# The in-place sums of weights of a decoder layer move from VectorE to GpSimd

## The chip, the cores and the metric

The kernel runs on one core of one Trainium2 chip. The metric is the device time of one execution in microseconds. The core's engines have their own instruction queues: TensorE (PE, its weight loads PEld), VectorE (DVE), ScalarE (ACT), GpSimd (POOL) and SyncE (SP). They wait for each other by semaphores. DMAs are issued from the queues of SP, ACT and POOL.

## The reference

One layer of a decoder for 512 tokens of width 1024, in float32:

```
h   = rmsnorm(x, ln1) @ w_in       # columns: GLA q,k,v,r, forget gate; 3 groups of attention q,k,v; 2 gates
A   = gated linear attention (4 heads, chunks of 64)  -> norm, silu gate, @ w_o_gla
B   = causal dilated windowed attention (3 groups of 4 heads), combined by softmax weights, @ w_o_attn
x  += (sigmoid(gA) * A + sigmoid(gB) * B) @ w_out
x  += relu(rmsnorm(x, ln2) @ w_mlp1)^2 @ w_mlp2      # 1024 -> 4096 -> 1024
x  += sigmoid(rmsnorm(x, ln3) @ w_pg) * (p @ w_pp)
out = rmsnorm(x, ln_f)
```

Nearly all of the work is products of 512 x 1024 activations with weights of 1024 rows or more.

## The kernel before, in words

**Products in three parts.** Each float32 operand is split into a rounded high part `hi` and a rest `lo`, and TensorE forms hi*hi + hi*lo + lo*hi. A weight operand is a tile of 128x1024. ScalarE makes its `hi` (L280), VectorE its `lo` = w - `hi` (L275, both operands in SBUF).

**Seven products in place of eight.** Most weights are taken in groups in the manner of Strassen: four blocks A11, A21, A12, A22 give the seven weight operands A11, S1 = A21 + A22, A22, S2 = S1 + A11, A12, S4 = S2 + A12 and S3 = A11 + A21. `strassen` runs the seven stages in the order of STAGES, one operand a stage, 24 products of 256 columns each; `wide` does the same with two tiles per operand (S2.0, S2.1 and so on) and products of 512 columns. There are 22 groups of the first kind (k1, q2, k2, v0, gq, gk, gb0, gb1, ga0, ga1, m1q0 to m1q7 for w_mlp1, and m2s0c1, m2s1c1, m2s0c3, m2s1c3 for w_mlp2) and 3 of the second (v12, gv, r).

**How the sums are made.** S1 is one DMA from SP and a second from POOL that adds onto it (L242). S2 and S4 are made in place in S1's buffer by VectorE: in `sums`, L254 and L260 for the first kind, L251 for `wide`. S3 is made in A11's buffer by an adding DMA from POOL (L257), after S2 has read A11. There are 22 + 22 + 12 = 56 sums of 128x1024.

**What sets the order.** The schedule is written out by hand: each engine runs its instructions in the order in which the program issues them. All operands stand in one list. When TensorE comes to operand i, `weight` calls `fetch` up to i + 2, and one round of `fetch` for operand j issues the `lo` of j, the `hi` of j + 1, the sum of j + 2 and the loads for j + 3. There are five buffers for `hi`, four for `lo` and six for raw weights. So a sum is issued right behind a `lo`, on the engine's queue ahead of what follows, and the next rounds' `hi` waits for it. Behind the main products, `step` runs queues of side work (`side`, `later`) in small pieces: attention, norms, splits of activations (ScalarE L428, VectorE L436), evacuation of PSUM (ScalarE L368, VectorE L421), transposes of attention probabilities (TensorE L925) with their evacuation (ScalarE L917, out of four PSUM buffers `sm`).

Of the kernel before, what the change touches and what calls it, by code (L numbers as in the profile page):

```python
# [14 lines left out]
OP = mybir.AluOpType  # L15
# [165 lines left out]
def block_kernel(ctx, tc, xT, ws, pT, wts, wha, wa2, vec, lnf, rel, onehot, ident_d, mask_d, out):  # L181
    nc = tc.nc
    V, S, TE, SY, GP = nc.vector, nc.scalar, nc.tensor, nc.sync, nc.gpsimd
# [45 lines left out]
    ready, raw = {}, {}  # L229
# [16 lines left out]
    def sums(i):  # L246
        q, _, what = OPERANDS[i].partition(".")
        if what[:3] in ("S2.", "S4."):
            a, b = ("S1", "A11") if what[1] == "2" else ("S2", "A12")
            w = raw[OPERANDS[i]] = raw[f"{q}.{a}{what[2:]}"]  # L250
            V.tensor_tensor(w, w, raw[f"{q}.{b}{what[2:]}"], op=OP.add)  # L251
        elif what == "S2":
            w = raw[f"{q}.S2"] = raw[f"{q}.S1"]
            V.tensor_tensor(w, w, raw[f"{q}.A11"], op=OP.add)  # L254

            w = raw[f"{q}.S3"] = raw[f"{q}.A11"]
            GP.dma_start(w, wts[UNIT[f"{q}.A21"]], accum_op=OP.add)  # L257
        elif what == "S4":
            w = raw[f"{q}.S4"] = raw[f"{q}.S2"]
            V.tensor_tensor(w, w, raw[f"{q}.A12"], op=OP.add)  # L260

    def split_weights(tag, i, bufs):

# [4 lines left out]
    def fetch(upto):  # L268

        while done[0] < min(upto, len(OPERANDS) - 1):  # L270
            i = done[0] = done[0] + 1
            if i >= 0:
                w, hi = ready[OPERANDS[i]]
                lo = split_weights("lo", i, NW - 1)
                V.tensor_tensor(lo, w, hi.bitcast(F32), op=OP.subtract)  # L275
                ready[OPERANDS[i]] = (hi, lo)
            if 0 <= i + 1 < len(OPERANDS):
                w = raw[OPERANDS[i + 1]]
                hi = split_weights("hi", i + 1, NW)
                S.activation(hi, w, AF.Copy)  # L280
                ready[OPERANDS[i + 1]] = (w, hi)
            if 0 <= i + 2 < len(OPERANDS):
                sums(i + 2)
            if 0 <= i + 3 < len(OPERANDS):
                prepare(i + 3)
# [295 lines left out]
    def xsums():  # L581
# [12 lines left out]
        def splits(name, ts):  # L594
# [4 lines left out]
            yield  # L599

        yield from sums(lambda g, p, o: V.tensor_tensor(t1[g][:, o], x(g, p, 0, 0), x(g, p, 0, 1), op=OP.subtract))
        yield from splits("T1", t1)
        yield from sums(lambda g, p, o: minus(t2[g][:, o], t1[g][:, o], x(g, p, 1, 1)))
        yield from sums(lambda g, p, o: minus(t4[g][:, o], t2[g][:, o], x(g, p, 1, 0)))
        yield from splits("T4", t4)
# [1109 lines left out]
```

## Time and profile before

| | |
|---|---|
| timed runs | 958.70 and 958.91 us, median 958.81 |
| profiled execution | span 957.1 us from first to last instruction, 1.7 below that median |
| PE busy | 948.8 us (99%) |
| DVE busy | 739.4 us (77%) |
| ACT busy | 542.1 us (57%) |
| POOL busy | 95.4 us (10%) |
| L251, L254 and L260 on DVE | 14.7 + 27.0 + 26.9 = 68.6 us |

The rows of the profile give line, engine, operation, out<-in by tile name, shapes and count, then busy time, mean ns of one, and the idle time of the engine just before. In a timeline a row gives start and length in us, and in brackets the idle time before it and what ended it. The chain that ended last is followed back from the last instruction, at each step to what released it.

### The profile page before, as it was taken

Reading aid. Unit: us, or ns where it says so; the run is one execution under the profiler, and the core shown is the slowest. Engines: PE = TensorE matmul, PEld = TensorE weight load, DVE = VectorE, ACT = ScalarE, POOL = GpSimd, SP = SyncE. Lnnn points to the kernel's source line nnn. Section 1 sums busy time; section 2 is a strip of 40 time slices with the busy share of each in tenths; the row PEclk is TensorE's granted clock in tenths of the full one; section 3 lists DMA queues with packets and bytes.
Section 4 is the critical chain, followed back from the end, with each engine's and each line's share of the span. In section 5 each row is a group of like instructions: output and inputs, shape, how many; then the busy total and the mean of one; then the engine's idle time right before and its main releaser. Section 6 shows DMA issues by size and latency. Waiting matters only on the chain.

```text
span 957.1 us, 15729 instructions
## 1 busy us (share of the span) xinstructions
PE 948.8 (99%) x6230; PEld 868.7 (91%) x6230; DVE 739.4 (77%) x1060; ACT 542.1 (57%) x884; POOL 95.4 (10%) x135
## 2 busy tenths in 40 slices
PE   9999999999999999999999999999999999999997
PEld 8789998899988888999988899999998998988886
DVE  7698879866788689969765798777677899787754
ACT  7357547545674679675723456556566673354733
POOL 0140010130000012031010000101000100000000
PEclk9999999999999999999999999999999999999999
DMA  9384472973738647465645436565653473563102
GB/s 323 123 238 119 118 177 67 315 232 98 173 70 256 153 128 185 112 140 192 176 107 193 120 77 188 136 169 156 170 148 105 124 185 99 140 189 102 45 1 89
DMA packets 43722, 142.00 MB, mean 148 GB/s; under 512 B 6467, under 2 KB 7055, under 8 KB 43648
## 3 DMA queue, kind: packets, MB, share of 16 engines
q1 hardware_dynamic: 28512, 96.42, 30.2%
q0 software_dynamic: 11456, 40.07, 21.2%
q10 hardware_dynamic: 3680, 4.51, 1.3%
q8 instruction: 49, 0.80, 0.4%
q14 instruction: 25, 0.20, 0.1%
HBM read 134.64 MB, written 8.17 MB: 149 GB/s over the span
## 4 chain that ended last, share of the span: by engine, by line
PE 96%; DVE 1%; ACT 1%; issue 1%; DMA 0%; POOLq 0%; POOL 0%; DVEq 0%; ACTq 0%
PE mmt L294 81%; PE smt L294 6%; PE mmt L551 2%; PE smt L985 1%; PE smt L925 1%; PE smt L848 1%; DVE ur L436 1%; PE smt L942 0%; PE smt L818 0%; PE smt L931 0%; PE smt L817 0%; PE smt L941 0%; PE smt L1548 0%; PE smt L1141 0%; PE smt L1041 0%
## 5 line engine op out<-in xcount | busy, mean ns | idle before, releaser
L294 PE MATMUL mmt<-ur,hi 128*128 128x256 f32 (+1 forms) x2896 | 594.7, 303 | 0.0
L294 PEld LDWEIGHTS mmt<-ur,hi 128*128 128x128 f32 x2896 | 466.0, 188 | 21.9
L294 PE MATMUL mmt<-ur,lo 128*128 128x256 f32 (+1 forms) x1448 | 438.9, 303 | 0.0
L275 DVE TENSOR_TENSOR lo<-w,hi 128x1024 fp32r<-128x1024 f32 x250 | 303.9, 1221 | 52.3 <-PE mmt L294 30.1
L280 ACT ACTIVATE hi<-w 128x1024 fp32r<-128x1024 f32 x250 | 261.2, 1054 | 103.9 <-PE mmt L294 31.6
L294 PEld LDWEIGHTS mmt<-ur,lo 128*128 128x128 f32 x1448 | 272.7, 188 | 10.8
L294 PE MATMUL mmt<-hi,ur 128*128 128x512 f32 (+3 forms) x576 | 162.5, 367 | 0.0
L428 ACT ACTIVATE ur<-u 128x512 fp32r<-128x512 f32 x122 | 72.3, 624 | 97.2 <-DVE u L1249 30.9
L294 PEld LDWEIGHTS mmt<-hi,ur 128*128 128x128 f32 x576 | 102.5, 188 | 15.8
L294 PE MATMUL mmt<-lo,ur 128*128 128x512 f32 (+3 forms) x288 | 105.0, 365 | 0.0
L421 DVE TENSOR_TENSOR u<-u,mmt 128x512 f32<-128x512 f32 (+1 forms) x112 | 70.3, 656 | 36.2 <-PE mmt L294 35.9
L436 DVE TENSOR_TENSOR ur<-u,ur 128x512 fp32r<-128x512 f32 x121 | 79.7, 689 | 16.6 <-ACT ur L428 16.2
L368 ACT ACTIVATE u<-mmt 128x512 f32<-128x512 f32 x80 | 47.5, 594 | 47.6 <-PE mmt L294 47.2
L242 POOL DMA_DIRECT2D w<-in_wts_dram x34 | 31.3, 960 | 334.6 <-DMA w<-in_wts_dram 181.4
L294 PEld LDWEIGHTS mmt<-lo,ur 128*128 128x128 f32 x288 | 54.2, 188 | 8.5
L257 POOL DMA_DIRECT2D w<-in_wts_dram x22 | 19.7, 894 | 316.7 <-DVE w L254 227.4
L294 PE MATMUL smt<-ur,hi 128*128 128x512 f32 x160 | 50.4, 393 | 0.1
L294 PEld LDWEIGHTS smt<-ur,hi 128*128 128x128 f32 x160 | 29.7, 188 | 8.0 <-PE smt L648 0.8
L294 PE MATMUL smt<-ur,lo 128*128 128x512 f32 x80 | 31.2, 390 | 0.0
L254 DVE TENSOR_TENSOR w<-w 128x1024 f32<-128x1024 f32 x22 | 27.0, 1225 | 0.8
L260 DVE TENSOR_TENSOR w<-w 128x1024 f32<-128x1024 f32 x22 | 26.9, 1225 | 0.8
L461 ACT ACTIVATE u<-u 128x512 f32<-128x512 f32 x24 | 14.9, 621 | 16.7 <-DVE u L1330 16.7
(214 smaller groups left out, 791.7 us busy)
## 6 DMA issues: line engine op xcount, KB each, us to landing
w<-in_wts_dram SPq DMA_DIRECT2D x172, 512.0 KB, 4.4
w<-in_wts_dram POOLq DMA_DIRECT2D x56, 512.0 KB, 5.9
u<-in_xT_dram SPq DMA_DIRECT2D x8, 256.0 KB, 5.3
u<-in_ws_dram SPq DMA_DIRECT2D x8, 256.0 KB, 5.5
v_dram<-u ACTq DMA_DIRECT2D x8, 256.0 KB, 9.0
u<-v_dram POOLq DMA_DIRECT2D x8, 256.0 KB, 6.6
y_dram<-u ACTq DMA_DIRECT2D x8, 256.0 KB, 3.9
u<-y_dram POOLq DMA_DIRECT2D x8, 256.0 KB, 6.1
```

What stands on the lines that cost most here:

```text
L242: GP.dma_start(w, wts[UNIT[b]], accum_op=OP.add)
L254: V.tensor_tensor(w, w, raw[f"{q}.A11"], op=OP.add)
L257: GP.dma_start(w, wts[UNIT[f"{q}.A21"]], accum_op=OP.add)
L260: V.tensor_tensor(w, w, raw[f"{q}.A12"], op=OP.add)
L275: V.tensor_tensor(lo, w, hi.bitcast(F32), op=OP.subtract)
L280: S.activation(hi, w, AF.Copy)
L294: TE.matmul(o, lhsT=l, rhs=r, start=a, stop=b, skip_group_check=shared)
L368: S.activation(sums[c], bank[b], AF.Copy, scale=-scale if c[0] else scale)
L421: V.tensor_tensor(out, s, ps, op=OP.subtract if m else OP.add)
L428: S.activation(hi, x, AF.Copy)
L436: V.tensor_tensor(lo, x, hi.bitcast(F32), op=OP.subtract)
L551: TE.matmul(q0ps[i], lhsT=(hi, hi, lo)[j][:, c], rhs=(xh, xl, xh)[j], start=not k and not j, stop=k == KC - 1 and j == 2)
```

## The change

The three calls in `sums` are issued to GpSimd instead of VectorE. Nothing else is changed: operands, buffers and the place in the program's order are the same.

```
@@ def sums(i)
         if what[:3] in ("S2.", "S4."):
             ...
-            V.tensor_tensor(w, w, raw[f"{q}.{b}{what[2:]}"], op=OP.add)
+            GP.tensor_tensor(w, w, raw[f"{q}.{b}{what[2:]}"], op=OP.add)
         elif what == "S2":
             w = raw[f"{q}.S2"] = raw[f"{q}.S1"]
-            V.tensor_tensor(w, w, raw[f"{q}.A11"], op=OP.add)
+            GP.tensor_tensor(w, w, raw[f"{q}.A11"], op=OP.add)
             ...
         elif what == "S4":
             w = raw[f"{q}.S4"] = raw[f"{q}.S2"]
-            V.tensor_tensor(w, w, raw[f"{q}.A12"], op=OP.add)
+            GP.tensor_tensor(w, w, raw[f"{q}.A12"], op=OP.add)
```

On VectorE in group m1q0, the first of w_mlp1, around the sum of S4 (ur are split activations, lo split weights, w raw weights):

```order
 L436 TENSOR_TENSOR ur<-u,ur 128x512
 L275 TENSOR_TENSOR lo<-w,hi 128x1024
-L260 TENSOR_TENSOR w<-w 128x1024
 L436 TENSOR_TENSOR ur<-u,ur 128x512 x2
 L275 TENSOR_TENSOR lo<-w,hi 128x1024
```

The sum between the `lo` of S2 and the next two splits is gone, and the splits and the `lo` of A12 follow at once.

On VectorE in group m2s0c1, the first seven-product group of w_mlp2, around the sum of S2:

```order
 L436 TENSOR_TENSOR ur<-u,ur 128x512 x4
 L275 TENSOR_TENSOR lo<-w,hi 128x1024
-L254 TENSOR_TENSOR w<-w 128x1024
 L436 TENSOR_TENSOR ur<-u,ur 128x512 x2
 L275 TENSOR_TENSOR lo<-w,hi 128x1024
```

Here the sum behind the `lo` of S1 is gone.

On GpSimd from the end of the attention's first part to group gq: L888 and L889 carry the attention's softmax weights through DRAM, L242 adds the second half of the next group's S1, L257 makes S3:

```order
 L779 DMA u<-v_dram 128x512 x8
 L888 DMA k_dram<-u 16x128
 L889 DMA cc<-k_dram 128x4x4
 L242 DMA w<-in_wts_dram 128x1024
-L257 DMA w<-in_wts_dram 128x1024 x2
-L242 DMA w<-in_wts_dram 128x1024 x4
+L254 TENSOR_TENSOR w<-w 128x1024
+L257 DMA w<-in_wts_dram 128x1024
+L260 TENSOR_TENSOR w<-w 128x1024
+L254 TENSOR_TENSOR w<-w 128x1024
```

The sum of gq's S2 (the first L254) now stands behind those DMAs in one queue, and later DMAs stand behind sums.

More of the change, by code (lines that the diff above doesn't have):

```diff
@@ L250, in sums @@
             w = raw[OPERANDS[i]] = raw[f"{q}.{a}{what[2:]}"]
-            V.tensor_tensor(w, w, raw[f"{q}.{b}{what[2:]}"], op=OP.add)
+            GP.tensor_tensor(w, w, raw[f"{q}.{b}{what[2:]}"], op=OP.add)
         elif what == "S2":
             w = raw[f"{q}.S2"] = raw[f"{q}.S1"]
-            V.tensor_tensor(w, w, raw[f"{q}.A11"], op=OP.add)
+            GP.tensor_tensor(w, w, raw[f"{q}.A11"], op=OP.add)
             w = raw[f"{q}.S3"] = raw[f"{q}.A11"]
@@ L259, in sums @@
             w = raw[f"{q}.S4"] = raw[f"{q}.S2"]
-            V.tensor_tensor(w, w, raw[f"{q}.A12"], op=OP.add)
+            GP.tensor_tensor(w, w, raw[f"{q}.A12"], op=OP.add)
     def split_weights(tag, i, bufs):
```

## The prediction

> **What bounds the kernel now.** I read the profile's page first: the busy shares, the chain that ended last, and the costliest groups.
>
> ```profile
> PE 948.8 (99%) x6230; PEld 868.7 (91%) x6230; DVE 739.4 (77%) x1060; ACT 542.1 (57%) x884; POOL 95.4 (10%) x135
> ...
> PE 96%; DVE 1%; ACT 1%; issue 1%; DMA 0%; POOLq 0%; POOL 0%; DVEq 0%; ACTq 0%
> ...
> L294 PE MATMUL mmt<-ur,hi 128*128 128x256 f32 (+1 forms) x2896 | 594.7, 303 | 0.0
> ...
> L254 DVE TENSOR_TENSOR w<-w 128x1024 f32<-128x1024 f32 x22 | 27.0, 1225 | 0.8
> ```
>
> TensorE holds 96% of the chain and its largest group has 0.0 us of idle time in front of it. The 56 sums cost VectorE 56 x 1.225 = 68.6 us, but VectorE is 1% of the chain. Taking its work away can give back almost nothing: the most would be that 1%, some 9 us, and most of that is not sums. So the question is only whether the weights still reach TensorE in time.
>
> How much time they have shows in the table by stretches of time, here for a run of seven-product groups:
>
> ```profile
> 640.00:720.00 80.00, 80.00 (x677) 80.00 (x676) 59.65 (x72) 48.22 (x71) 6.15 (x7) 1.00 0.60 159
> ```
>
> 677 products in 80 us are 118 ns each, so one stage of 24 products lasts 2.84 us and a group of seven 19.9 us. VectorE is busy 59.65/80, that is 14.9 us in 20. By the code `lo` has four buffers, so the `lo` of operand k may be written when stage k-4 has ended, and is needed three stages (8.5 us) later. The timeline of VectorE shows such a release:
>
> ```profile
> 693.07 1.23 DVE L275 TENSOR_TENSOR lo<-w,hi 128x1024 fp32r<-128x1024 f32 x1 [1.62 <-PE mmt L294]
> ...
> 696.93 1.22 DVE L275 TENSOR_TENSOR lo<-w,hi 128x1024 fp32r<-128x1024 f32 x1
> 698.18 1.22 DVE L254 TENSOR_TENSOR w<-w 128x1024 f32<-128x1024 f32 x1
> 699.33 0.68 DVE L421 TENSOR_TENSOR u<-u,mmt 128x512 f32<-128x512 f32 x1
> ```
>
> The first `lo` waited for PE, so it has the whole margin: 8.5 - 1.2 = 7.3 us. The next could have started at 693.07 + 2.84 = 695.9, starts at 696.93, and still has 6.3 us.
>
> **What a sum costs on GpSimd.** No row shows GpSimd reading 1024 columns. The nearest:
>
> ```profile
> L1592 POOL TENSOR_TENSOR fr<-sp,mh 128x1 f32<-128x1 f32 x4 | 2.2, 545 | 47.4 <-DVE sp L1591 47.4
> ...
> L525 POOL MEMSET u<- 128x512 f32 x1 | 0.5, 528 | 0.0
> ...
> L526 POOL MEMSET u<- 128x8 f32 x1 | 0.1, 111 | 0.1
> ```
>
> A two-input operation on one column takes 0.55 us, which I take as its fixed part. Writing 504 columns more takes 0.528 - 0.111 = 0.417 us, so a pass over 1024 columns 0.85 us. With reads and write side by side a sum is 0.55 + 0.85 = 1.4 us; with the two reads after one another 0.55 + 1.7 = 2.25; with the write after them 3.1. I take 2.3, the middle, and keep 1.4 and 3.1 as ends. [...]
>
> The second cost is that GpSimd and VectorE get in each other's way. GpSimd's small `pow` operations beside VectorE's rows:
>
> ```profile
> 341.37 0.72 POOL L456 TENSOR_TENSOR grs<-rv,mh 128x2 f32<-128x2 f32 x1 [2.81 <-DVE rv L455]
> ...
> 362.45 3.49 POOL L456 TENSOR_TENSOR grs<-rv,mh 128x2 f32<-128x2 f32 x2 [3.53 <-DVE rv L455]
> ...
> 412.25 1.54 POOL L456 TENSOR_TENSOR grs<-rv,mh 128x2 f32<-128x2 f32 x1 [2.71 <-DVE rv L455]
> ```
>
> ```profile
> 362.27 1.22 DVE L275 TENSOR_TENSOR lo<-w,hi 128x1024 fp32r<-128x1024 f32 x1
> 363.40 1.29 DVE L1213 TENSOR_TENSOR u<-u 128x512 f32<-128x512 f32 x2
> ...
> 412.01 1.22 DVE L275 TENSOR_TENSOR lo<-w,hi 128x1024 fp32r<-128x1024 f32 x1
> ```
>
> Undisturbed one takes 0.72 us. The one at 412.25 met a `lo` that ended at 413.23, and ended itself at 413.79, 0.56 later. The pair at 362.45 took 3.49 instead of 1.44: the first got through only after three VectorE operations in a row, at 364.69. So while VectorE reads two SBUF operands GpSimd waits, and VectorE's next such operation, if it is ready, goes first. Only operations with both operands in SBUF kept it out in these rows; one with an operand in PSUM (L421) I take to let it in. [...]
>
> **The change, part by part.**
>
> *Most groups: nothing.* In the rows at 696.93 the sum is ready at 698.15 and L421, which reads PSUM, stands behind it: GpSimd starts at once and ends at about 700.4, where VectorE ended at 699.40. One us late, plus a short wait for the next `lo`, against margins of 6 to 7 us. The accumulating DMA L257, which waits behind the sum in POOL's queue, goes out one us later too, and its result is split only four operands on. Worth 0. If the cover goes (VectorE behind by more than about 5 us), each sum costs TensorE what it is late.
>
> *Term C, the first group of w_mlp1 (m1q0).* TensorE's form changes to 256 columns where this group begins:
>
> ```profile
> 560.04 0.41 PE L294 MATMUL mmt<-ur,hi 128*128 128x256 f32 x2
> ...
> 567.11 1.22 DVE L275 TENSOR_TENSOR lo<-w,hi 128x1024 fp32r<-128x1024 f32 x1
> ...
> 570.70 1.22 DVE L275 TENSOR_TENSOR lo<-w,hi 128x1024 fp32r<-128x1024 f32 x1
> 571.84 1.29 DVE L436 TENSOR_TENSOR ur<-u,ur 128x512 fp32r<-128x512 f32 x2
> 573.04 3.49 DVE L275 TENSOR_TENSOR lo<-w,hi 128x1024 fp32r<-128x1024 f32 x3
> ...
> 569.67 1.06 ACT L280 ACTIVATE hi<-w 128x1024 fp32r<-128x1024 f32 x1 [0.22 <-DVE w L260]
> 570.64 0.58 ACT L368 ACTIVATE u<-mmt 128x512 f32<-128x512 f32 x1
> 571.12 0.62 ACT L428 ACTIVATE ur<-u 128x512 fp32r<-128x512 f32 x1
> ```
>
> S4 is the sixth stage, 560.04 + 5 x 2.84 = 574.2, its `lo` is needed 0.2 later and is ready at 574.26 now: no margin. Without the sum VectorE goes on at 568.33 with two L436, the `lo` of A12 and one L436, all of two SBUF operands, to about 571.3 (571.84 + 0.65 less the sum's 1.22). Its next L436 needs the L428 that stands in ScalarE's queue behind the `hi` that waits for the sum. There GpSimd gets in: 571.4 to 573.7; `hi` to 574.8, L368 and L428 to 576.1, L436 to 576.7, `lo` to 577.9 against about 574.5: **3.4 us**. If GpSimd is let in after the first L436 (569.0 to 571.3), VectorE pushes the `lo` of A12 to 573.1 against 571.7: 1.4 us, the lower end.
>
> *Term D, the first group of w_mlp2 (m2s0c1).*
>
> ```profile
> 743.51 0.41 PE L294 MATMUL mmt<-ur,hi 128*128 128x256 f32 x2
> ...
> 748.09 1.29 DVE L1392 TENSOR_TENSOR u<-u 128x512 f32<-128x512 f32 x2
> 749.54 1.31 DVE L436 TENSOR_TENSOR ur<-u,ur 128x512 fp32r<-128x512 f32 x2 [0.16 <-ACT ur L428]
> 750.77 1.22 DVE L275 TENSOR_TENSOR lo<-w,hi 128x1024 fp32r<-128x1024 f32 x1
> ...
> 744.72 1.06 ACT L280 ACTIVATE hi<-w 128x1024 fp32r<-128x1024 f32 x1 [1.81 <-DVE w L254]
> 748.87 1.26 ACT L428 ACTIVATE ur<-u 128x512 fp32r<-128x512 f32 x2 [3.09 <-DVE u L1392]
> ```
>
> S2 is the fourth stage: 743.51 + 8.5 = 752.0, `lo` at 752.3, ready now at 751.99. Without the sum VectorE runs two-input work until L1392 ends at 748.2, 1.2 earlier; then it needs the two L428, which stand behind the `hi` that waits for the sum. GpSimd: 748.2 to 750.5; `hi` to 751.6, L428 to 752.9, L436 to 753.5, `lo` to 754.7: **2.4 us** late. Let in at once it puts VectorE back by 2.3 - 1.2 = 1.1 us, less the 0.3 left: 0.8 us late.
>
> *Term A, the first sum of gq.* In POOL's queue it stands behind L889, which waits for a DMA, and L242.
>
> ```profile
> 204.61 1.06 ACT L280 ACTIVATE hi<-w 128x1024 fp32r<-128x1024 f32 x1 [2.26 <-DVE w L254]
> ...
> 210.52 0.49 ACT L917 ACTIVATE u<-smt 128x384 f32<-128x384 f32 x1
> ...
> 208.08 0.79 POOL L889 DMA_DIRECT2D cc<-k_dram  x1 [8.29 <-DMA k_dram<-u]
> 209.15 0.92 POOL L242 DMA_DIRECT2D w<-in_wts_dram  x1 [0.28 <-issue]
> ...
> 215.36 0.60 PE L925 MATMUL smt<-ident,u 128*128 128x128 f32 x4
> ```
>
> The `hi` that started at 204.61 cannot start before the sum ends, 209.7 + 2.3 = 212.0, or 214.3 if the L905 operations in between keep GpSimd out as well. ScalarE is blocked for 7.5 to 10 us, and L917, which empties the PSUM of the attention's transposes, comes after that `hi`, another and an L368: it ends at 215.3 to 217.6. The four `sm` buffers are full by then, so the fifth set of transposes (215.36) waits up to 2.2 us; the third L917 stands behind S4's `hi` and makes it 0.9 to 4.8 us in all. I take **3**.
>
> *Sum.* 3.4 + 2.4 + 3 = 8.8 us on the profiled execution's span of 957.1: 965.9. The timed runs have their median 1.7 us above that span (958.81), so **967.6 us**, 0.9% slower.
>
> **Rivals.**
>
> *The margins hold everywhere.* GpSimd is served between VectorE's operations and a sum takes 1.4 to 2.3 us: 1.4 + 0.8 + 0.9 = 3.1 us at most, 958.8 to 962. For it: margins of 6 to 7 us in most groups. Against: the pair at 362.45.
>
> *The two engines together become the bound.* If a sum blocks VectorE for its whole length, a group needs 14.9 - 2 x 1.22 = 12.4 us of VectorE and twice the sum. At 2.3 that is 17 us, below the 19.9 of TensorE; it decides from 3.75 us a sum. At 4.5 us a group takes 21.4, and 22 such groups add 33 us: 992 us. For it: the stretches between are fuller than this one. Against: not even the upper end of 3.1 reaches it, unless GpSimd's waits count too. [...]
>
> *VectorE's relief shows.* If GpSimd's sums disturb nobody, the few places where VectorE is late gain: at most part of its 1% of the chain, 955 to 958 us. Against: at those very places GpSimd is kept out.
>
> **How the numbers follow.** Likeliest case, local stalls, 962 to 975 (its upper end: 4.8 in A, and 3.1 us a sum, which adds 0.8 to C and D each and some stalls in the other groups with a late VectorE): 0.55. Margins hold: 0.23. Together the bound, over 976: 0.17. Relief: 0.05. The range leaves out the outer halves: 959 to 980. A difference under 2% (19 us) is about what a measurement of this kernel can't tell from no change: faster by over 2% has 0.01, slower 0.15, within 0.84.
>
> **What would show it.** Sums on POOL of about 2.3 us where VectorE pauses and longer where it doesn't; VectorE about 69 us less busy, or its `lo` rows longer if GpSimd blocks it; PE waiting for `lo` near 574 and 752 and for ScalarE near 215 to 222; L917 some 5 us later. Wrong would be: sums of over 3.75 us everywhere, `hi` waiting for POOL in every group with PE gaps behind it, or no gap of PE at all.

## The result, and the profile after

| | before | after |
|---|---|---|
| timed runs, first comparison | 958.70 and 958.91, median 958.81 us | 968.49 and 970.77, median 969.63 us |
| the same kernel again, five runs beside nine of before | median 958.88 us | 966.53 to 970.57, median 967.32 us |
| profiled execution | span 957.1 us | span 969.0 us, time 970.77 us |

The ratio is 1.0113 with a 95% interval of 1.0083 to 1.0142, and in the repetition 1.0092 (1.0079 to 1.0105): slower by 1%, and neither interval includes no change. The forecast was 967.6 us; 969.63 lies in the 962 to 975 us of its likeliest case.

The busy shares and the chain that ended last, from the page of the kernel after:

```profile
PE 953.9 (98%) x6230; PEld 871.6 (90%) x6230; DVE 739.0 (76%) x1004; ACT 538.7 (56%) x884; POOL 244.0 (25%) x191
...
PE 87%; DVE 5%; issue 3%; POOL 2%; ACT 2%; DMA 1%; POOLq 0%; DVEq 0%; ACTq 0%
```

TensorE has 87% of the chain in place of 96%. The striking number is VectorE's: 56 operations of 1.225 us are gone, and it is as busy as before, 739.0 against 739.4 us. Its remaining operations have taken up the 68 us. Three groups of VectorE before, the same three after, and the costliest groups of GpSimd after (busy, mean ns of one, idle time ahead):

```profile
L275 DVE TENSOR_TENSOR lo<-w,hi 128x1024 fp32r<-128x1024 f32 x250 | 303.9, 1221 | 52.3 <-PE mmt L294 30.1 <-ACT hi L280 16.8 <-issue 4.1
L436 DVE TENSOR_TENSOR ur<-u,ur 128x512 fp32r<-128x512 f32 x121 | 79.7, 689 | 16.6 <-ACT ur L428 16.2
...
L1347 DVE TENSOR_SCALAR u<-u 128x512 f32<-128x512 f32 x32 | 13.5, 424 | 0.5
```

```profile
L275 DVE TENSOR_TENSOR lo<-w,hi 128x1024 fp32r<-128x1024 f32 x250 | 332.3, 1336 | 50.5 <-ACT hi L280 33.5 <-PE mmt L294 12.3 <-issue 4.1
L436 DVE TENSOR_TENSOR ur<-u,ur 128x512 fp32r<-128x512 f32 x121 | 86.2, 741 | 19.2 <-ACT ur L428 18.8
...
L1347 DVE TENSOR_SCALAR u<-u 128x512 f32<-128x512 f32 x32 | 21.4, 671 | 0.5
```

```profile
L260 POOL TENSOR_TENSOR w<-w 128x1024 f32<-128x1024 f32 x22 | 60.4, 2746 | 77.9 <-DVE lo L275 51.3 <-ACT u L368 12.0 <-ACT ur L428 6.8
L254 POOL TENSOR_TENSOR w<-w 128x1024 f32<-128x1024 f32 x22 | 59.3, 2695 | 235.1 <-DVE lo L275 205.2 <-ACT u L461 22.1 <-DMA w<-in_wts_dram 7.8
```

A `lo` takes 1336 ns in the mean where it took 1221, an L436 741 where it took 689, an L1347 671 where it took 424. How that comes about shows in a steady group of w_mlp1, VectorE's row first and GpSimd's below it:

```profile
693.67 4.69 DVE L275 TENSOR_TENSOR lo<-w,hi 128x1024 fp32r<-128x1024 f32 x2
```

```profile
693.51 2.50 POOL L260 TENSOR_TENSOR w<-w 128x1024 f32<-128x1024 f32 x1 [2.99 <-DVE lo L275]
```

Two `lo` in a row take 4.69 us in place of some 2.4: the first does not get on until the sum ends at 696.01. TensorE has no wait there, so this costs nothing. Where TensorE does wait, the view of its waits says (us in total, times, longest):

```profile
PE smt L925 <- DVE u L905: 2.7, 1, 2.7
PE mmt L294 <- DVE lo L275: 1.9, 2, 1.0
PE mmt L294 <- ACT u L368: 1.6, 1, 1.6
```

With the starts of the 6230 products laid beside those of before, the profiled execution loses 12.0 us, all at five places: 4.3 in gq (212.7 to 217.0 us), 1.05 in gv (301 to 307), 1.1 in ga0 (449), 1.85 in m1q0 (574 to 581) and 3.7 in m2s0c1 (762.6 to 766.7). Three of them are shown row by row here. In gv TensorE waits 0.46 us for an L421 and in ga0 0.87 us for a `lo`; what made these late was not followed further.

**gq.** GpSimd, VectorE and TensorE, each from its own timeline:

```profile
207.03 0.80 POOL L889 DMA_DIRECT2D cc<-k_dram  x1 [8.39 <-DMA k_dram<-u]
208.08 0.90 POOL L242 DMA_DIRECT2D w<-in_wts_dram  x1 [0.25 <-issue]
208.67 2.70 POOL L254 TENSOR_TENSOR w<-w 128x1024 f32<-128x1024 f32 x1
```

```profile
208.43 4.03 DVE L275 TENSOR_TENSOR lo<-w,hi 128x1024 fp32r<-128x1024 f32 x1
212.39 2.04 DVE L905 TENSOR_SCALAR u<-u,cn 128x128 f32<-128x128 f32 x8
```

```profile
212.72 0.70 PE L925 MATMUL smt<-ident,u 128*128 128x128 f32 x3 [2.68 <-DVE u L905]
```

The sum stood behind L889 and came just when VectorE came with a `lo`. The `lo` waited for the whole sum, the L905 behind it waited for the `lo`, and TensorE stood 2.68 us for the first set of transposes.

**m1q0** (GpSimd, VectorE, TensorE):

```profile
576.06 2.70 POOL L260 TENSOR_TENSOR w<-w 128x1024 f32<-128x1024 f32 x1 [9.00 <-ACT u L368]
```

```profile
575.83 3.48 DVE L436 TENSOR_TENSOR ur<-u,ur 128x512 fp32r<-128x512 f32 x2
579.23 1.21 DVE L275 TENSOR_TENSOR lo<-w,hi 128x1024 fp32r<-128x1024 f32 x1
```

```profile
574.83 0.39 PE L294 MATMUL mmt<-ur,hi 128*128 128x256 f32 x1 [0.34 <-DVE ur L436]
580.50 0.39 PE L294 MATMUL mmt<-ur,lo 128*128 128x256 f32 x1 [1.01 <-DVE lo L275]
```

GpSimd got in between the two L436, and the second had to wait: 3.48 us for a pair that takes 1.29. That is the wait at 580.50. The one at 574.83 goes back to S2's sum of the same group, which met a VectorE operation with one SBUF input (GpSimd, VectorE):

```profile
563.46 2.39 POOL L254 TENSOR_TENSOR w<-w 128x1024 f32<-128x1024 f32 x1 [22.14 <-ACT u L461]
```

```profile
563.23 2.77 DVE L1293 TENSOR_SCALAR u<-u,cv 128x256 f32<-128x256 f32 x2
```

The pair took 0.61 us before. VectorE gains the 1.22 us of the sum that it no longer makes, loses 2.16 here, and is about 0.9 us late from there on.

**m2s0c1** (GpSimd, VectorE, TensorE):

```profile
752.16 6.87 POOL L254 TENSOR_TENSOR w<-w 128x1024 f32<-128x1024 f32 x1 [21.86 <-DVE lo L275]
```

```profile
751.93 1.29 DVE L436 TENSOR_TENSOR ur<-u,ur 128x512 fp32r<-128x512 f32 x2
753.14 1.22 DVE L275 TENSOR_TENSOR lo<-w,hi 128x1024 fp32r<-128x1024 f32 x1
754.27 1.29 DVE L436 TENSOR_TENSOR ur<-u,ur 128x512 fp32r<-128x512 f32 x2
755.48 1.29 DVE L1392 TENSOR_TENSOR u<-u 128x512 f32<-128x512 f32 x2
760.67 1.29 DVE L436 TENSOR_TENSOR ur<-u,ur 128x512 fp32r<-128x512 f32 x2 [3.90 <-ACT ur L428]
```

```profile
762.64 0.50 PE L294 MATMUL mmt<-ur,hi 128*128 128x256 f32 x2 [1.64 <-ACT u L368]
```

Here it is GpSimd that is kept out. VectorE runs seven two-input operations without a pause until 756.77, none of them any longer than alone, and the sum ends 2.26 us after that.

### The profile page after: what moved, and what is told of

Same layout as the page of the kernel before. It is cut to its first block, busy times and chain, and to the rows that moved or that the text cites. A ratio compares the mean times of both kernels' runs of the same rounds, so it can differ in the third digit from the quotient of the medians.

```text
span 969.0 us, 15751 instructions
## 1 busy us (share of the span) xinstructions
PE 953.9 (98%) x6230; PEld 871.6 (90%) x6230; DVE 739.0 (76%) x1004; ACT 538.7 (56%) x884; POOL 244.0 (25%) x191
## 4 chain that ended last, share of the span: by engine, by line
PE 87%; DVE 5%; issue 3%; POOL 2%; ACT 2%; DMA 1%; POOLq 0%; DVEq 0%; ACTq 0%
PE mmt L294 72%; PE smt L294 6%; PE mmt L551 2%; DVE lo L275 2%; POOL w L254 1%; PE smt L925 1%; POOL w L260 1%; PE smt L985 1%; DVE ur L436 1%; PE smt L848 1%; DMA u<-y_dram 1%; ACT ur L428 1%; ACT hi L280 0%; PE smt L523 0%; DVE u L421 0%
## 5 line engine op out<-in xcount | busy, mean ns | idle before, releaser
L275 DVE TENSOR_TENSOR lo<-w,hi 128x1024 fp32r<-128x1024 f32 x250 | 332.3, 1336 | 50.5 <-ACT hi L280 33.5
L428 ACT ACTIVATE ur<-u 128x512 fp32r<-128x512 f32 x122 | 72.1, 624 | 100.4 <-DVE u L1249 30.9
L254 POOL TENSOR_TENSOR w<-w 128x1024 f32<-128x1024 f32 x22 | 59.3, 2695 | 235.1 <-DVE lo L275 205.2
L421 DVE TENSOR_TENSOR u<-u,mmt 128x512 f32<-128x512 f32 (+1 forms) x112 | 70.2, 654 | 40.7 <-PE mmt L294 40.6
L436 DVE TENSOR_TENSOR ur<-u,ur 128x512 fp32r<-128x512 f32 x121 | 86.2, 741 | 19.2 <-ACT ur L428 18.8
L260 POOL TENSOR_TENSOR w<-w 128x1024 f32<-128x1024 f32 x22 | 60.4, 2746 | 77.9 <-DVE lo L275 51.3
L242 POOL DMA_DIRECT2D w<-in_wts_dram x34 | 30.6, 925 | 163.5 <-DMA w<-in_wts_dram 97.4
L368 ACT ACTIVATE u<-mmt 128x512 f32<-128x512 f32 x80 | 47.3, 591 | 25.8 <-PE mmt L294 25.7
L251 POOL TENSOR_TENSOR w<-w 128x1024 f32<-128x1024 f32 x12 | 31.2, 2597 | 46.0 <-DVE lo L275 46.0
```

Of the source, the lines that this page charges most:

```text
L242: GP.dma_start(w, wts[UNIT[b]], accum_op=OP.add)
L251: GP.tensor_tensor(w, w, raw[f"{q}.{b}{what[2:]}"], op=OP.add)
L254: GP.tensor_tensor(w, w, raw[f"{q}.A11"], op=OP.add)
L260: GP.tensor_tensor(w, w, raw[f"{q}.A12"], op=OP.add)
L368: S.activation(sums[c], bank[b], AF.Copy, scale=-scale if c[0] else scale)
L421: V.tensor_tensor(out, s, ps, op=OP.subtract if m else OP.add)
```

## The experiments

The theory: the loss is made at these five places alone, by a sum that comes late or holds VectorE up where the weights have no margin. The main rivals: every sum costs a little; it is the sum's length wherever it stands; GpSimd does not hold VectorE up at all and the sums are merely late. In the kernels with an edit ahead of a line, its number is 1 to 9 higher than above; the tile names tell it.

**Nine sums back on VectorE, and those nine alone on GpSimd.**

```
+        E = V if OPERANDS[i] in ("gq.S2", "gv.S4.0", "gv.S4.1", "ga0.S2", "ga0.S4",
+                                 "m1q0.S2", "m1q0.S4", "m2s0c1.S2", "m2s0c1.S4") else GP
-            GP.tensor_tensor(w, w, ...)
+            E.tensor_tensor(w, w, ...)          # in all three places
```

> Nine sums go back to VectorE: S2 of gq, both S4 of gv, S2 and S4 of ga0, of m1q0 and of m2s0c1. The other 47 stay on GpSimd. Theory (the whole loss is made at these five places, where the weights have no margin): the loss of 10.8 us is gone, 958.8 to 960.5 us, though VectorE's lo rows stay longer than 1.22 us beside the 47 sums. Rival (every sum costs TensorE a little, 10.8 / 56 = 0.19 us each): 47 x 0.19 = 9.1 us stay, 967.9 us.

The second kernel has `GP` and `V` exchanged in the first line.

> Only those nine sums are on GpSimd, 47 are on VectorE as before. Theory (local stalls): nearly the whole loss, 968 to 970.5 us, with TensorE waiting at the same five places. Rival (spread evenly): 9 x 0.19 = 1.7 us, 960.5 us.

With the nine back: 959.01 us against 959.11 of before, ratio 1.000 (0.9991 to 1.0009). With the nine alone: 969.18 us, ratio 1.0107 (1.0091 to 1.0122). The whole loss hangs on 9 of 56 sums; the other 47 cost nothing, though they hold VectorE up as before. This kernel is no faster than the one before either, and no version here is. Three of the nine sums are put back one at a time below; the other six were tried only together with the rest of the nine. The page and the group of `lo` of the first kernel:

```profile
PE 949.1 (99%) x6230; PEld 869.1 (91%) x6230; DVE 736.2 (77%) x1013; ACT 539.0 (56%) x884; POOL 214.8 (22%) x182
...
L276 DVE TENSOR_TENSOR lo<-w,hi 128x1024 fp32r<-128x1024 f32 x250 | 329.2, 1323 | 47.0 <-ACT hi L281 26.7 <-PE mmt L295 15.8 <-issue 4.1
```

A `lo` of 1323 ns with no microsecond lost: VectorE's longer rows are covered by the margins.

**One sum back, in gq.**

```
+        E = V if OPERANDS[i] == "gq.S2" else GP
```

> One sum goes back to VectorE, S2 of gq. The trace of the changed kernel has 4.3 us of the loss between 212.7 and 217.0 us. Theory (this one sum makes them): 969.6 - 4.3 = 965.3 us, 964.3 to 966.3. Rival (the place is late anyway and the stall passes to the next sum of gq): 968 us or more.

965.33 us (964.66 to 966.21), ratio 1.0064 (1.0052 to 1.0077). In its trace TensorE has no wait in gq: the 4.3 us are gone and nothing takes their place. That the time meets the expectation to 0.03 us is luck, as single times of the changed kernel lie up to 4 us apart (see its repetition below).

**The same sum, on GpSimd but not behind L889.**

```
-        GP.dma_start(cc, k_dram.rearrange("h (m c) -> m h c", c=4))
-        for _ in range(4):
+        for _ in range(8):
             yield
+        GP.dma_start(cc, k_dram.rearrange("h (m c) -> m h c", c=4))
```

> All 56 sums on GpSimd. The second small DMA of the attention's softmax weights (L889 in the changed kernel) is issued eight steps of the side work later, so that the sum of gq's S2 stands ahead of it in GpSimd's queue; the attention's products start four steps later for it. Theory (the sum was late because it stood behind that DMA's wait until 207.0 us, and met VectorE's lo at 208.4): the sum runs from about 203.4 to 206 us while VectorE pauses, and the 4.3 us at 212.7 to 217.0 are gone: 965.3 us, 964 to 966.5. [...]

966.27 us, ratio 1.0074 (1.0061 to 1.0086). GpSimd and VectorE in gq:

```profile
203.23 2.38 POOL L254 TENSOR_TENSOR w<-w 128x1024 f32<-128x1024 f32 x1 [4.26 <-DVE lo L275]
```

```profile
208.21 1.22 DVE L275 TENSOR_TENSOR lo<-w,hi 128x1024 fp32r<-128x1024 f32 x1
209.34 2.05 DVE L905 TENSOR_SCALAR u<-u,cn 128x128 f32<-128x128 f32 x8
```

The sum runs alone in 2.38 us, the `lo` takes 1.22, and the wait in gq is gone. About 0.6 us are lost anew around 218.6, where TensorE waits 0.39 us for an L917; this is probably the price of the later attention, which the edit moves too. So in gq it was the place in GpSimd's queue that decided when the sum met the `lo`; the waits compared with the repetition below say the same.

**GpSimd beside VectorE, with nobody waiting for its results.** Three kernels, each from the kernel before:

```
+    scr = const.tile([P, 512], F32, name="scr")      # and PAD = 64 in place of 128
+    def beside(w):
+        for a in range(2):
+            GP.tensor_tensor(scr, w[:, a * 512:a * 512 + 512], scr, op=OP.add)
             V.tensor_tensor(w, w, ..., op=OP.add)
+            beside(w)                                 # behind each of the 56 sums
```

> The sums stay on VectorE as before. Behind each of the 56 GpSimd adds the two halves of the sum (128x512 each) onto a scratch tile that nobody else reads, so no engine waits for GpSimd; the split tiles' padding is cut from 128 to 64 columns to make room. Theory (GpSimd reading SBUF holds up VectorE's operations with two SBUF operands): VectorE's busy time rises by 40 to 80 us over the 739 of before, in the rows of L275, L436 and the like, and the time by 1 to 8 us at the places without margin: 960 to 967 us. Rival (no hold-up, the loss in the changed kernel is only that the sums come late): VectorE within 5 us of 739, 958.5 to 959.7 us.

The second has `GP.tensor_scalar(scr, w[...], 1.0, None, op0=OP.mult)` in its place, the third `GP.memset(scr, 0.0)`.

> As the kernel before, with two GpSimd multiplications by 1 of the halves of each sum into the same scratch tile: one SBUF operand in place of two. Theory (any GpSimd read of SBUF holds VectorE's two-operand rows up, for as long as it lasts): VectorE's busy time rises too, in proportion to what these rows take on GpSimd, by 20 to 60 us; 959.5 to 964 us. Rival (only GpSimd operations with two operands do it): VectorE within 5 us of 739, 958.5 to 959.7 us.

> As the kernel before, with two GpSimd memsets of the scratch tile (128x512 each) at the same 56 places in the program: they write and read nothing, and wait for nothing but GpSimd's own queue. It is also the control for the smaller padding. Theory (it is the read that is shared): VectorE within 5 us of 739, 958.5 to 959.7 us. Rival (any GpSimd work beside VectorE holds it up): VectorE 20 us busier or more, over 959.7 us.

The times: 984.48 us (ratio 1.0267, 1.025 to 1.0284), 968.7 us (1.01, 1.0085 to 1.0115) and 960.52 us (1.0016, 1.0006 to 1.0025). All three are above what was expected. VectorE's busy time in the three pages rises by 77.3, 22.1 and 10.4 us, where 40 to 80, 20 to 60 and at most 5 were expected:

```profile
PE 958.3 (97%) x6230; PEld 874.0 (89%) x6230; DVE 816.7 (83%) x1060; ACT 539.1 (55%) x884; POOL 276.3 (28%) x248
```

```profile
PE 952.4 (99%) x6230; PEld 869.8 (90%) x6230; DVE 761.5 (79%) x1060; ACT 541.8 (56%) x884; POOL 288.1 (30%) x248
```

```profile
PE 950.1 (99%) x6230; PEld 869.5 (91%) x6230; DVE 749.8 (78%) x1060; ACT 541.3 (56%) x884; POOL 154.7 (16%) x248
```

So the hold-up is shown by itself: VectorE's own work is that of before, nothing waits for a result of GpSimd, and VectorE's rows grow by 77 us. (One kind of wait there is, as S4's sum and later loads overwrite buffers that GpSimd reads: VectorE stood 1.2 us for it in the first kernel and 1.4 in the second, SyncE's loads 5.6 and 8.0 us. Waits are not part of the busy time.) The groups of VectorE in the third kernel tell which rows feel a GpSimd that only writes:

```profile
L284 DVE TENSOR_TENSOR lo<-w,hi 128x1024 fp32r<-128x1024 f32 x250 | 302.8, 1218 | 42.8 <-ACT hi L289 18.7 <-PE mmt L303 17.1 <-issue 5.8
L445 DVE TENSOR_TENSOR ur<-u,ur 128x512 fp32r<-128x512 f32 x121 | 79.5, 686 | 16.6 <-ACT ur L437 16.2
...
L1356 DVE TENSOR_SCALAR u<-u 128x512 f32<-128x512 f32 x32 | 20.8, 651 | 0.5
```

The operations with two SBUF operands do not feel it (1218 and 686 ns, against 1221 and 689). The TENSOR_SCALAR over 512 columns, 424 ns before, does: 651 ns, where the second kernel, with the same padding, has 439. Neither theory had that, and why it is so is not shown. By the mean of a `lo`, 1392 ns in the first kernel, 1258 in the second and 1218 in the third, VectorE's rows of two SBUF operands are held up by a GpSimd that reads SBUF and not by one that only writes. How long a hold-up lasts shows in gq, in the kernel after: the sum ended at 211.37 and the `lo` 1.09 us later, so the `lo` was held for the whole sum, but its row starts at 208.43, 0.24 us ahead of the sum's. Which of two that come almost together goes first stays open.

On the time all three expectations were too low. In the first kernel those of TensorE's waits that name VectorE add up to 13.4 us, `lo` first (us in total, times, longest):

```profile
PE mmt L303 <- DVE lo L284: 6.0, 4, 2.1
```

VectorE has its own sums and the hold-ups, and the margins no longer cover everything. In the third kernel 1.2 of the 2.0 us between its first product and its last are lost in gq; memsets and padding can't be told apart in it. In the second 4.95 of 7.8 us are lost in ga0. 1.7 of these are TensorE's granted clock: its mean in this execution is 0.996 and in that of before 0.998, which over 965.3 us makes 1.9 (what a fall of the clock costs is worked out with the repetition below). The rest starts in GpSimd's queue: the DMAs L1242 (L1233 before) stand behind two of the added operations. The rows, of before and of this kernel:

```profile
428.23 4.09 POOL L1233 DMA_DIRECT2D u<-y_dram  x7
```

```profile
433.78 4.09 POOL L1242 DMA_DIRECT2D u<-y_dram  x7
```

They go out 5.5 us later, where TensorE was only 1.8 us behind. In the first kernel the mean clock is 0.990, which makes by the same reckoning some 8 of its 25.7 us ((0.998 - 0.990) x 982.9 = 7.9); how much of the rest is queue and how much hold-up stays open.

**Each sum in four pieces.**

```
-            GP.tensor_tensor(w, w, x, op=OP.add)
+            for c in range(0, 1024, 256):
+                GP.tensor_tensor(w[:, c:c + 256], w[:, c:c + 256], x[:, c:c + 256], op=OP.add)
```

> All 56 sums on GpSimd as in the changed kernel, each as four operations of 128x256. Theory (the hold-up goes by the instruction, so VectorE gets in between the pieces): no lo row of VectorE is held for a whole sum, L275 falls from a mean of 1336 to 1250 to 1300 ns, but the four pieces take 3 to 4 us beside a busy VectorE in place of 2.4 to 2.7; the stall in gq shrinks, the ones of m1q0 and m2s0c1, where the sum itself is late, grow: 967 to 973 us. Rival (the pieces follow each other so closely that VectorE gets no turn): L275 at 1336 or more and 969 us or more.

976.37 us, ratio 1.0177 (1.0161 to 1.0193), above the range. VectorE and GpSimd:

```profile
L278 DVE TENSOR_TENSOR lo<-w,hi 128x1024 fp32r<-128x1024 f32 x250 | 319.9, 1286 | 82.4 <-ACT hi L283 74.4 <-PE mmt L297 4.0 <-issue 3.6
```

```profile
L263 POOL TENSOR_TENSOR w<-w 128x256 f32<-128x256 f32 x88 | 86.3, 1022 | 50.0 <-DVE lo L278 30.3 <-ACT u L371 10.6 <-ACT ur L431 5.1
```

The mechanism was right: VectorE gets in between, a `lo` falls to 1286 ns and VectorE is busy for 713.9 us, 25 less than before; no other version on GpSimd freed it of more than 5. But a sum takes 4 x 1.0 = 4 us in place of 2.7, the `hi` behind it come later (`lo` waits 74.4 us for them in all, 33.5 in the kernel after), and ga0 loses 4.0 us, m1q0 3.5 and m2s0c1 4.1, of which a fall of the clock makes 1.7 in ga0 and 1.7 in m2s0c1 (its mean is 0.994, and (0.998 - 0.994) x 972.1 = 3.9). gq loses 2.2 us, which is no less than the changed kernel loses there when the clock stays full (2.0, see its repetition below): the smaller stall that was expected there did not come.

**One sum back in m2s0c1, one in m1q0, and the changed kernel again.**

```
+        E = V if OPERANDS[i] == "m2s0c1.S2" else GP        # and "m1q0.S4" in the second
```

> One sum goes back to VectorE, S2 of m2s0c1, which took 6.87 us on GpSimd. The changed kernel loses 3.7 us between 762.6 and 766.7 us. Theory (this sum, kept out by VectorE's row of two-operand work, makes them): 969.6 - 3.7 = 965.9 us, 964.9 to 967. Rival (the next sum of the group, S4 with 3.23 us, is late too and takes the stall over): 968 us or more.

> One sum goes back to VectorE, S4 of m1q0. The changed kernel loses 1.85 us between 574.1 and 580.5 us. Theory (this sum holds VectorE's L436 up by 2.07 us and so the lo of A12 behind it): 969.6 - 1.85 = 967.8 us, 966.8 to 968.8. Rival (VectorE comes late to this group whatever S4 does, as with its own sum there was no margin either): 969 us or more.

> The changed kernel once more, for the spread of its time beside the kernel before. Theory (the wait of the small DMA L889 ends after 6.4 us in one execution and 8.4 in another, and with it the stall in gq is 0.8 or 4.3 us): single times between 966 and 971 us, median 969 to 970. Rival (the spread has no place of its own): all within 0.3% of one another, 968.2 to 971.

966.36 us (1.0074, 1.0061 to 1.0088), 967.46 us (1.0091, 1.0078 to 1.0105), and 967.32 us for the changed kernel itself. The first two were reckoned from 969.6, and beside 967.32 their medians show little. Place by place the traces are clear. Without m2s0c1's S2 on GpSimd the 3.7 us there are gone. Without m1q0's S4, 0.9 of the 1.85 stay: the wait of 1.01 us at 580.50 is gone and the one for L436 is not. S2's sum is still on GpSimd in this kernel, and still holds the same TENSOR_SCALAR up, for 2.50 us, so the rest belongs to it.

The repetition's median is below the 969 to 970 us that was expected, and it shows where the spread is. It lost 2.0 us in gq where the first execution lost 4.3, and 2.2 in m2s0c1 where that lost 3.7, while the waits themselves differ by only 0.8 us in gq and not at all in m2s0c1 (1.90 and 1.68 us against 2.68 and 1.64). The difference is TensorE's granted clock, the number behind GpSimd's busy time in the table by stretches. Of the kernel after, behind the wait in gq and behind the one in m2s0c1:

```profile
213.00:216.00 3.00, 3.00 (x18) 3.00 (x18) 3.00 (x9) 1.72 (x4) 0.00 (x0) 0.60 0.96 153
216.00:220.00 4.00, 4.00 (x32) 4.00 (x32) 4.00 (x8) 1.43 (x3) 2.40 (x1) 0.87 0.46 147
...
762.00:764.00 2.00, 1.34 (x6) 1.14 (x7) 2.00 (x2) 0.59 (x2) 0.75 (x1) 0.79 0.99 195
764.00:766.00 2.00, 2.00 (x11) 2.00 (x11) 0.24 (x1) 0.00 (x0) 2.00 (x1) 0.50 0.06 12
766.00:768.00 2.00, 2.00 (x17) 2.00 (x17) 0.40 (x1) 1.49 (x3) 0.48 (x1) 0.86 0.33 33
```

Of its repetition, where m2s0c1's wait ended at 759.88:

```profile
762.00:764.00 2.00, 2.00 (x19) 2.00 (x19) 0.00 (x0) 0.24 (x1) 1.73 (x1) 1.00 0.00 0
```

At 0.50 there are 11 products in 2 us in place of 19. In steps of 0.2 us the clock of the kernel after reads 0.50 from 213.8 to 217.0 and from 763.2 to 766.4, 1.00 around these stretches, and 0.53 to 0.94 in the steps at their ends. So the rows give 0.4 x 3 / 0.5 + 0.13 x 4 / 0.5 = 3.4 us at half in gq and (0.21 + 0.50 + 0.14) x 2 / 0.5 = 3.4 us in m2s0c1, and so 1.7 us lost at each. The theory of the spread, the wait of L889, holds only in part. The row of that DMA in the kernel with nine sums on GpSimd, and in the repetition:

```profile
204.68 0.79 POOL L890 DMA_DIRECT2D cc<-k_dram  x1 [6.44 <-DMA k_dram<-u]
```

```profile
206.25 0.80 POOL L889 DMA_DIRECT2D cc<-k_dram  x1 [8.17 <-DMA k_dram<-u]
```

In the first TensorE's wait in gq was only 0.70 us. Over the five traces in which this sum, undivided, stands behind that DMA, the DMA goes out at 204.7, 206.3, 206.6, 207.0 and 207.0 us, and TensorE waits 0.70, 1.90, 2.45, 2.90 and 2.68 us, so the wait does follow it. But in the second L889 waited nearly as long as the 8.39 us of the first execution, and the time was 4 us lower. The five executions of the repetition have spans of 964.8, 964.8, 965.5 and 965.8 us at a mean clock of 0.998, and 968.8 at 0.995: most of the spread is the clock.

## Why the prediction was right, point by point

**The bound.** TensorE stayed the bound and VectorE's lighter list gave nothing back. It could not, and for a second reason that the prediction named only as an alternative: VectorE is not less busy, since what it saves (68.6 us) comes back as longer rows beside GpSimd's sums (68.2 us: 739.0 - 739.4 + 68.6).

**The price of a sum.** Taken as 2.3 us between 1.4 and 3.1; alone it is 2.38, as in the row at 203.23.

**Who keeps whom out.** From the rows of before I had that GpSimd waits for VectorE and that VectorE's next ready operation goes first. m2s0c1 shows this (6.87 us). That L421, with an operand in PSUM, lets GpSimd in was assumed; in the kernel after an L421 of 0.69 us at 687.42 lies within a sum of 2.38 us at 686.94, and neither is longer than alone. The other half, VectorE blocked by GpSimd, stood in no row of before, and the lower ends of C and D and the rival of the two engines supposed it for a sum's whole length. The runs show 2.3 us on the two `lo` of the steady group, beside a sum of 2.50. It entered none of the three terms' likeliest values.

**Most groups cost nothing.** Right: 47 sums, 959.01 us.

**Term A, gq, 3 us.** Measured 2.0 and 4.3 in the two profiled executions, with the clock at full and at half. The place in the queue behind L889 was the cause, as the experiment with L889 shows. That 3 lies between the two is luck, as the path was another: I had ScalarE blocked behind `hi` and its L917 keeping PSUM full, and the wait was VectorE's, a `lo` held by the sum with L905 behind it. TensorE waited at the first transposes, not at the fifth.

**Term C, m1q0, 3.4 us.** The step that was mis-sized. I let VectorE run on to the last L436; but its second L436 had to wait for an L428 anyway, GpSimd came in there, which is the path that the prediction kept for its lower end, and S4's sum cost 0.9 us, below even that end of 1.4. Another 0.9 came from S2 of the same group, which I had not priced.

**Term D, m2s0c1, 2.4 us.** Right in mechanism and size: the sum ended 2.3 us after VectorE's row of two-input work, and the loss was 2.2 us without the fall of the clock, 3.7 with it. TensorE's last releaser was ScalarE's L368, which stands behind the late `hi`, and not `lo`.

**What was left out.** gv and ga0, 1.05 and 1.1 us, which I had only in the upper end; and the clock, 1.7 us a stall. Without the clock gq, m1q0, m2s0c1 and these two places together measure 2.0 + 1.85 + 2.2 + 2.0 = 8.0 us beside the sum of 8.8. A was 1.0 too large, C 1.55 and D 0.2, and the two places that I left out make up 2.0 of that. That the sum came out so near is luck; that the losses are local stalls, at the three places named, is not.

**The rivals.** The margins did not hold at the three places named. The two engines together were not the bound: a sum took 2.7 us, below the 3.75 from which that decides, and no run shows the 4.5 us behind its 992 as a mean (L251, L254 and L260 have 2.60 to 2.75). The first of the kernels with added GpSimd work goes some way towards it, with VectorE at 817 us and 984 us in all. There was no relief.

## What to carry to other kernels

Moving an elementwise operation over two SBUF operands from VectorE to GpSimd need not free VectorE of anything when both are busy: here 68.6 us left and 68.2 came back as longer rows, and each sum took 2.4 to 6.9 us in place of 1.2. What the move cost was decided at the few places without margin, so look there for what stands ahead of the moved operation in its new queue and behind it, and for what the other engine runs at that moment. Moving only the other 47 sums cost nothing here, and gained nothing (959.01 against 959.11 us). Cutting the operation into pieces let VectorE in but made a sum half as long again, which was worse where its result was waited for.

## What the runs showed of the hardware

TensorE's granted clock fell to half for 3.4 us (0.50 in the rows by stretches above) after waits of only 1.6 to 2.9 us, and not every time: in the profiled executions of the kernels with sums on GpSimd, 9 of the 11 such waits in gq and m2s0c1 were followed by it. Why the two of the repetition, 1.90 and 1.68 us long, were not, when one of 1.64 us was, stays open. A memset on GpSimd, which reads nothing, lengthened VectorE's TENSOR_SCALAR from 424 to 651 ns and left its operations with two SBUF operands alone (1218 and 686 ns against 1221 and 689). GpSimd's one-operand multiplication took longer than its two-operand add, 1.74 against 1.65 us for 512 columns in the mean.
